# Second gate's modulation on VectorE inside the down projection, instead of on TensorE, with new queue orders

## The chip, the cores and the metric

The kernel runs on one core of one Trainium2 chip. A core has five engines that run side by side and wait for each other by semaphores: TensorE (PE, matrix products; its weight loads are shown apart as PEld), VectorE (DVE), ScalarE (ACT), GpSimd (POOL) and SyncE (SP), which here issues the DMA transfers. The metric is the device time of one execution in microseconds (us), lower is better.

## What is computed

One layer of a hybrid diffusion backbone on 128 context tokens and 512 latent tokens, with a model width D of 1024 and a feed-forward width of 2816. The input vectors `c` (latent) and `c_ctx` (context) are turned into six modulation vectors of 1024 each; the last one, `g2`, scales the output of the feed-forward part. Cut to what matters here:

```python
mod = silu(cond) @ w_ada + b_ada              # cond: c for latent tokens, c_ctx for context tokens
sh1, sc1, g1, sh2, sc2, g2 = split(mod, 6)
...                                           # token mixing: input projection, SSD and convolution, output projection
x = x + g1 * rms_norm(mix, norm_mix_post)

h = rms_norm(x, norm_ffn_pre) * (1 + sc2) + sh2
up = h @ w_ffn_up                             # 1024 -> 5632
up = depthwise_conv3x3(up)                    # latent tokens on a grid of 8 x 64; context: 3 taps in a row
f_gate, f_val = split(up, 2)
f = (silu(f_gate) * f_val) @ w_ffn_down       # 2816 -> 1024
x = x + g2 * rms_norm(f, norm_ffn_post)
```

So `g2` is used only at the very end, where the feed-forward output is scaled, and as a vector per kind of token.

## The kernel before

**Layout.** Channels lie on the 128 partitions, the 640 tokens (512 latent, then 128 context) along the free axis. The model width is 8 tiles of 128, the feed-forward width 22 tiles. Columns are handled in two halves where a norm forces it: 384 first, 256 last (`HC`). All products are made of two-part operands: a number is split into a high part (a rounded copy, made by ACT) and a low part (the rest, a subtraction by POOL or DVE), and three products high x high, high x low, low x high are added up in PSUM (`mm3`).

**Weights** come in units of 128 x 1024 or 128 x 768. For each unit SP issues one load into a tile `wr` (two buffers, L287), ACT makes `wh` (L311), POOL makes `wl` (L313). Units are numbered in order of use: `wr67` is the third unit of the up projection, `wr121` the first unit of output tile 4 of the down projection (tiles are counted from 0).

**Modulation.** `ada_first` and `ada_half` make it on PE: the weights of 512 outputs (8 tiles of 128x512, loaded by `ada_load`, L452) are multiplied by silu(c) and silu(c_ctx) in 32 matmuls (L460; two rows of the trace each), copied by ACT (L463), transposed by PE (L423), and added to the bias by DVE (L432) into `modv`. Halves 6 and 7 are `g2`. In the kernel before, half 6 is made in the up projection's head, half 7 after its unit 11.

**Up projection** (about 485 to 840 us). The head takes five units, first for the first 384 columns, then, when the second half of the norm is done, for the last 256 (L1259); the residual's second half (`xr`, L1247) is loaded meanwhile. Then one unit after another: 48 matmuls into one of three PSUM buffers, then the 3x3 convolution straight from PSUM: ACT makes the centre tap (L1227), DVE adds eight taps and two more for the context (L1237, L1239, L1240). `finish` multiplies gate and value (L1333, L1339); `split_f` splits the product for the down projection (L400 on ACT, L402 on DVE or POOL).

**Down projection** (about 820 to 960 us). Eight output tiles, each 22 x 3 products over the columns; PE only needs weights and the split products. The first two tiles are interleaved: their first 16 products come before the last six, since the last products are ready late. `down_out` has ACT square the result (L1412) and copy it, scaled by `gg2` (g2 times the norm's weight), into `mg` (L1418): tile 0 and 1 into slots H5 and H6, 2 and 3 into S8 and S9, 4 to 7 into S16, S17, U0 and U1.

**Tail** (960 to 979 us). For each half of the columns the sums of squares are made on PE, the root on ACT and DVE (L487, L488), spread by PE and copied by ACT into `HL` (L1437). `out_apply` multiplies each of the eight tiles by it (L1446), adds the residual (L1447) and sends the tile (L1448): tiles 0, 3 and 6 on POOL, the others on DVE.

**What sets the order.** The order of the instructions within each engine's queue (PE, DVE, ACT, POOL, SP) is written out: the table `ORDER` gives, for each engine, the numbers of its instructions (in the order in which the code makes them) in the order in which they are to be issued. An engine issues in that order and stops at the first instruction whose inputs or buffers aren't ready.

## Time and profile before

| | before |
|---|---|
| time, median of 3 runs (us) | 981.96 |
| lowest and highest | 980.89, 983.74 |
| span of the profiled execution, first to last instruction | 979.4 |
| mean granted TensorE clock | 0.996 |
| busy: PE, PEld, DVE, ACT, POOL (us) | 944.5, 920.9, 686.9, 471.3, 577.9 |
| moved by DMA (MB) | 117.52 |

The profiled execution's own time is its span, 979.4, with what lies around the first and last instruction; the median of the runs is 2.6 above it. Rows of the timeline read: start in us, length in us, engine, line, operation, what it writes and reads, partitions and elements, count; in brackets the idle time of the engine before it and what ended it. Neighbouring instructions of one form are one row (x4), and its length goes from the first start to the last end. "SPq" rows are the times at which SP issues a DMA. In the windows each row is a stretch: from and to, its length, then the busy time (and count) of PE, PEld, DVE, ACT and POOL, the granted TensorE clock, the share of the DMA engines and GB/s.

### The profile page before, as it was taken

How to read it: one execution, taken by the hardware profiler on the slowest of the kernel's cores; microseconds unless marked ns; L12 is line 12 of the kernel's file. 1: busy time of each engine (PE TensorE's matmuls, PEld its weight loads, DVE VectorE, ACT ScalarE, POOL GpSimd, SP SyncE). 2: the span in 40 equal slices, each digit the busy share in tenths (PEclk: the TensorE clock that was granted, in tenths of full speed). 3: DMA queues.
4: the chain of work that ended last, by engine and by line, in shares of the span. 5: the costliest groups of instructions: out<-in, count | busy, mean ns of one | idle time of the engine just before them, and what ended most of it. 6: DMA issues, size and time to landing. Idle time of an engine off the chain costs nothing.

```text
span 979.4 us, 18795 instructions
## 1 busy us (share of the span) xinstructions
PE 944.5 (96%) x7623; PEld 920.9 (94%) x7623; DVE 686.9 (70%) x1076; ACT 471.3 (48%) x799; POOL 577.9 (59%) x416
## 2 busy tenths in 40 slices
PE   4999999999999999999999999999999999999995
PEld 3799999999999998998889999999999999999995
DVE  1769898999989997523585998998988898400004
ACT  4355666877668477622464852323232336322211
POOL 1334699889999882534662994444454436543434
PEclk9999999999999999999999999999999999999998
DMA  9622424433424422578662322222222231322213
GB/s 347 250 72 86 117 82 127 146 95 123 139 80 142 128 91 93 196 244 303 200 218 88 129 86 69 84 78 73 86 66 86 66 87 54 94 69 76 82 38 108
DMA packets 50294, 117.52 MB, mean 120 GB/s; under 512 B 6016, under 2 KB 13952, under 8 KB 50208
## 3 DMA queue, kind: packets, MB, share of 16 engines
q1 hardware_dynamic: 50208, 116.33, 37.2%
q8 instruction: 60, 0.98, 0.4%
q14 instruction: 26, 0.21, 0.1%
HBM read 112.55 MB, written 3.75 MB: 119 GB/s over the span
## 4 chain that ended last, share of the span: by engine, by line
PE 87%; DMA 3%; ACT 3%; DVE 2%; SPq 1%; POOL 1%; issue 1%; POOLq 0%; ACTq 0%; DVEq 0%
PE ps L415 72%; PE ps L1259 3%; PE pq L415 2%; PE pq L818 2%; PE pq L807 1%; PE pq L460 1%; SPq L452 1%; DMA wr<-in_wout 1%; PE pq L744 1%; PE pq L441 1%; POOL wl L313 1%; PE pq L473 1%; DMA S<-acD 1%; ACT wh L311 1%; DMA T<-in_wada 1%
## 5 line engine op out<-in xcount | busy, mean ns | idle before, releaser
L313 POOL TENSOR_TENSOR wl<-wr,wh 128x1024 fp32r<-128x1024 f32 (+3 forms) x127 | 290.4, 2290 | 316.3 <-ACT wh L311 299.2
L415 PE MATMUL ps<-H,wh 128*128 128x384 f32 (+1 forms) x1636 | 315.7, 309 | 0.1
L311 ACT ACTIVATE wh<-wr 128x1024 fp32r<-128x1024 f32 (+3 forms) x131 | 131.3, 1003 | 316.2 <-PE ps L415 183.2
L415 PE MATMUL ps<-T,wh 128*128 128x384 f32 (+1 forms) x1472 | 272.5, 306 | 1.8 <-ACT S L1227 1.8
L1237 DVE SCALAR_TENSOR_TENSOR S<-ps,prms,S 128x441 f32<-128x441 f32 (+2 forms) x336 | 233.5, 695 | 29.4 <-ACT S L1227 18.9
L415 PEld LDWEIGHTS ps<-H,wh 128*128 128x128 f32 x1636 | 249.0, 188 | 2.7 <-issue 1.7
L415 PEld LDWEIGHTS ps<-T,wh 128*128 128x128 f32 x1472 | 218.9, 188 | 2.2 <-ACT S L1227 2.1
L872 DVE SCALAR_TENSOR_TENSOR ps<-u,prms,ps 128x655 f32<-128x655 f32 x205 | 185.1, 903 | 10.8 <-ACT ps L869 4.8
L415 PE MATMUL ps<-H,wl 128*128 128x384 f32 (+1 forms) x818 | 191.8, 309 | 0.0
L415 PE MATMUL ps<-T,wl 128*128 128x384 f32 (+1 forms) x736 | 166.2, 305 | 0.0
L415 PEld LDWEIGHTS ps<-H,wl 128*128 128x128 f32 x818 | 129.0, 188 | 1.0 <-issue 1.0
L415 PEld LDWEIGHTS ps<-T,wl 128*128 128x128 f32 x736 | 113.0, 188 | 0.0
L488 DVE RECIPROCAL rsm<-rsm 128x160 f32<-128x160 f32 (+2 forms) x9 | 7.4, 817 | 147.1 <-ACT rsm L487 147.1
L415 PE MATMUL ps<-S,wh 128*128 128x384 f32 (+1 forms) x420 | 88.0, 310 | 1.6 <-ACT wh L311 1.6
L415 PEld LDWEIGHTS ps<-S,wh 128*128 128x128 f32 x420 | 66.5, 188 | 2.8 <-ACT wh L311 1.8
L415 PE MATMUL ps<-S,wl 128*128 128x384 f32 (+1 forms) x210 | 54.9, 309 | 0.3 <-POOL wl L313 0.3
L789 ACT ACTIVATE S<-S,AC 128x128 f32<-128x128 f32 x140 | 45.5, 392 | 2.4 <-DMA S<-acD 2.4
L885 POOL TENSOR_TENSOR T<-T,T 128x640 f32<-128x640 f32 x20 | 32.0, 1602 | 12.5 <-ACT T L881 12.5
L1227 ACT ACTIVATE S<-ps,prms 128x640 f32<-128x640 f32 x42 | 36.5, 869 | 0.0
L415 PEld LDWEIGHTS ps<-S,wl 128*128 128x128 f32 x210 | 35.2, 188 | 0.9 <-POOL wl L313 0.5
L881 ACT ACTIVATE T<-u,prms 128x512 f32<-128x512 f32 (+1 forms) x54 | 27.9, 554 | 6.8 <-POOL T L885 6.8
L1339 POOL TENSOR_TENSOR H<-S,S 128x640 f32<-128x640 f32 x16 | 25.3, 1581 | 0.0
(346 smaller groups left out, 1180.3 us busy)
## 6 DMA issues: line engine op xcount, KB each, us to landing
wr<-in_wup SPq DMA_DIRECT2D x44, 512.0 KB, 3.5
wr<-in_win SPq DMA_DIRECT2D x36, 512.0 KB, 3.9
T<-in_wada SPq DMA_DIRECT2D x49, 256.0 KB, 5.4
S<-acD SPq DMA_DIRECT2D x28, 320.0 KB, 4.7
wr<-in_wdown SPq DMA_DIRECT2D x16, 512.0 KB, 3.4
wr<-in_wout SPq DMA_DIRECT2D x13, 512.0 KB, 4.5
H<-in_wada SPq DMA_DIRECT2D x23, 256.0 KB, 4.6
S<-in_wada SPq DMA_DIRECT2D x16, 256.0 KB, 5.4
```

The source lines that it names most:

```text
L311: ac.activation(hi[:, :n], raw[:, :n], AF.Copy)
L313: lo_eng.tensor_tensor(lo[:, :n], raw[:, :n], hi[:, :n].bitcast(F32), SUB)
L415: last_mm[0] = te.matmul(out, w, x[:, c0:c1], start=first and i == 0, stop=last and i == 2)
L789: ac.activation(rc, rc, AF.Relu, scale=-1.0, bias=AC2[:, c, row:row + 1])
L818: te.matmul(py[64 * h:64 * h + 64, i * P:(i + 1) * P], xt[:, c * P + 64 * h:c * P + 64 * h + 64], rs[h, d][:, c * P:(c + 1) * P], start=d ...
L872: ve.scalar_tensor_tensor(acc, u[:, j:j + UO], w(j), acc, MUL, ADD)
L881: ac.activation(t[:, b:c], u[:, a:a + c - b], AF.Copy, scale=w(j))
L885: gp.tensor_tensor(far, far, t, ADD)
L1227: ac.activation(out, v, AF.Identity, bias=prm_col("ffn_b", i), scale=w(1, 1))
L1237: ve.scalar_tensor_tensor(ob, vl[:, r0 + a - 1:r1 + a - 1, q0 + b - 1:q1 + b - 1], w(a, b), ob, MUL, ADD)
L1259: te.matmul(pt[:, o:o + c1 - c0], w[k] if i in (1, 2) else w[:, k * P:(k + 1) * P], x[:, c0:c1], start=k == 0 and j == 0, stop=k == KD - 1 ...
L1339: gp.tensor_tensor(f_raw[q], a, b, MUL)
```

## The change

The two last calls of `ada_half` (6 and 7) and their loads go. Instead:

- `w_ada`'s columns of g2 are laid out transposed in memory, one row of 1024 inputs per output channel, as two tiles of 128x512 for each of the eight output tiles.
- `cond_rows`, called in the up projection, loads c and c_ctx as rows broadcast to all 128 partitions (four transfers of 128x512 into S16, S17, U0 and U1) and has ACT make their silu.
- `gate_load(m)` loads the two weight tiles of output tile m: tile 0 into H5 and H6, the others into S8 and S9, one after the other. `gate_rows(m)` has DVE multiply them by the rows and sum along the free axis (`accum_out`): four operations of 128x512, then two small ones for bias and norm weight. It then issues the loads of tile m + 1.
- These are called from the down projection when its weight units come up (units 1, 3, 4, 5, 6 and 7 in `DOWN_ORDER`).
- The tables of `ORDER` are written anew from the up projection on, for DVE, ACT, POOL and SP also where nothing was added. PE's order stays as it was, apart from the matmuls that go.

```diff
-    sy.dma_start(ids, idhl_d)
+    sy.dma_start(ids, idhl_d[0:P, :])
...
-    ada_w2 = ada_load(6, [f"S{k}" for k in range(8)])
...
-    ada_half(6, ada_w2)
...
+    def cond_rows():
+        for c in range(2):
+            for h in range(2):
+                t = slot(("S16", "S17", "U0", "U1")[2 * c + h])[:, 0:512]
+                src = idhl_d[P + 32 * c + 16 * h:P + 32 * c + 16 * h + 16, :].rearrange("a b -> (a b)")
+                sy.dma_start(t, src.unsqueeze(0).to_broadcast([P, 512]))
+                ac.activation(t, t, AF.Silu)
+                crows.append(t)
...
-        if i == 11:
-            g2_rest = ada_half(7, ada_w2, now=False)
-        if i == 14:
-            g2_rest()
-        if i == 5:
-            ada_w2 = ada_load(7, [f"H{8 + k}" for k in range(8)])
+        if i == 32:
+            cond_rows()
...
-    ve.tensor_tensor(gg2, modv[:, 40:48, :], prm_col("g_ffn_post", 0, 8).unsqueeze(2).to_broadcast([P, 8, 2]), MUL)
+    junk = sm.tile([P, T], F32, tag="tanh", name="junk", bufs=1)
+    gate_ws = []
+
+    def gate_load(m):
+        ws = []
+        for h in range(2):
+            t = slot((("S8", "S9") if m else ("H5", "H6"))[h])
+            sy.dma_start(t[:, 0:512], wada2[6 + m // 4, 2 * (m % 4) + h])
+            ws.append(t)
+        gate_ws.append(ws)
+
+    def gate_rows(m):
+        for c in range(2):
+            for h, w in enumerate(gate_ws[m]):
+                ve.scalar_tensor_tensor(junk[:, 0:512], w[:, 0:512], 1.0, crows[2 * c + h], MUL, MUL,
+                                        accum_out=modv[:, 2 * m + h, c:c + 1])
+        ve.scalar_tensor_tensor(modv[:, 40 + m, :], modv[:, 2 * m, :], prm_col("b_ada", 40 + m), modv[:, 2 * m + 1, :],
+                                ADD, ADD)
+        ve.tensor_scalar(gg2[:, m, :], modv[:, 40 + m, :], prm_col("g_ffn_post", m), None, MUL)
+        if 0 < m < KD - 1:
+            gate_load(m + 1)
...
+                i = DOWN_ORDER.index((m, g))
+                if i == 1:
+                    gate_load(0)
+                    gate_load(1)
+                for j in {3: (0,), 4: (1,), 5: (2, 3), 6: (4, 5), 7: (6, 7)}.get(i, ()):
+                    gate_rows(j)
...
+    g2 = a["w_ada"][0][:, 5 * D:].T.reshape(KD, P, 2, 512).transpose(0, 2, 1, 3).reshape(2, KD, P, 512)
+    out["wada2"] = np.concatenate([w2[0:6], g2])
```

Of the tables in `ORDER`, one line of SP's:

```diff
-275 277 279 284 281 283 285-343 345 344 346 348 347 349 351 350 353 352 354 356 355 357 359 358""",
+348 357-358 360-361 363 351 354 356 359 362""",
```

What the tables do at three places follows; the numbers at the names tell buffers apart, and line numbers of the changed kernel are one higher here (L288 for L287, L403 for L402, L1479 and L1480 for L1446 and L1447).

SP's queue at the start of the up projection, before. `wr66` to `wr69` are weight units, `xr` the residual's second half, `S1` to `S3` weights of half 6 of the modulation.

```order
L452 DMA S1_636_5941<-in_wada2 128x512 [waits DMAHW3_49]
L287 DMA wr66_5893<-in_wup 128x1024 [waits DMAHW0_49,Activation_49,Pool_49]
L287 DMA wr67_5955<-in_wup 128x1024 [waits DMAHW1_49,Pool_49]
L1247 DMA xr_626_5926<-in_xT 128x2x256 [waits PE_49]
L1247 DMA xr_628_5930<-in_xT 128x2x256 [waits DMAHW7_49,PE_49]
L1247 DMA xr_627_5928<-in_xT 128x2x256 [waits PE_49]
L287 DMA wr68_5961<-in_wup 128x1024 [waits DMAHW4_49,Pool_49]
L287 DMA wr69_5971<-in_wup 128x1024 [waits DMAHW5_49,DMAHW2_49,Pool_49]
```

The same place in the changed kernel:

```order
L288 DMA wr65_5878<-in_wup 128x1024 [waits DMAHW6_49,DMAHW1_49,Pool_49]
L288 DMA wr66_5893<-in_wup 128x1024 [waits DMAHW0_49,DMAHW2_49,Activation_49,Pool_49]
L1248 DMA xr_626_5926<-in_xT 128x2x256 [waits DMAHW3_49,PE_49]
L1248 DMA xr_628_5930<-in_xT 128x2x256 [waits PE_49]
L1248 DMA xr_627_5928<-in_xT 128x2x256 [waits PE_49]
L288 DMA wr67_5939<-in_wup 128x1024 [waits DMAHW1_49,Pool_49]
L288 DMA wr68_5945<-in_wup 128x1024 [waits DMAHW7_49,DMAHW2_49,Pool_49]
L288 DMA wr69_5955<-in_wup 128x1024 [waits DMAHW6_49,Pool_49]
```

The load of `wr67` now stands behind the three of `xr`; the loads of half 6 are gone.

DVE's queue at the end of the up projection, before: the end of the convolution into S11, four low parts (the right operands H2, H4, H0 and H8 are the high parts), and the start of the last convolution, into S13.

```order
L1239 SCALAR_TENSOR_TENSOR S11_807_9251<-ps0_797_9131,prms_105,S11_807_9251 128x127
L1240 SCALAR_TENSOR_TENSOR S11_807_9251<-ps0_797_9131,prms_105,S11_807_9251 128x127 [waits DVE_49]
L402 TENSOR_TENSOR H3_817_9281<-H10_756_8027,H2_816_9279 128x640 [waits Activation_49]
L402 TENSOR_TENSOR H7_819_9285<-H11_761_8164,H4_818_9283 128x640 [waits Activation_49]
L402 TENSOR_TENSOR H1_821_9289<-H12_766_8301,H0_820_9287 128x640 [waits Activation_49,Pool_49]
L402 TENSOR_TENSOR H9_823_9293<-H13_771_8438,H8_822_9291 128x640 [waits DMAHW0_49,Activation_49,Pool_49]
L1237 SCALAR_TENSOR_TENSOR S13_824_9295<-ps1_798_9186,prms_105,S13_824_9295 128x7x63 [waits PE_49]
```

The same place in the changed kernel (`junk` is the accumulation of gate 0; the six taps between the first and the last into S13 are left out):

```order
L1410 SCALAR_TENSOR_TENSOR junk_9239,modv_123<-H5_825_9304,S16_754_8399 128x512 [waits DMAHW5_49]
L403 TENSOR_TENSOR H3_801_9185<-H10_736_7919,H2_800_9183 128x640 [waits Activation_49]
L403 TENSOR_TENSOR H7_803_9189<-H11_741_8056,H4_802_9187 128x640 [waits Activation_49]
L403 TENSOR_TENSOR H1_805_9193<-H12_746_8193,H0_804_9191 128x640 [waits Activation_49,Pool_49]
L1238 SCALAR_TENSOR_TENSOR S13_808_9199<-ps1_782_9090,prms_105,S13_808_9199 128x7x63 [waits PE_49,Activation_49]
L1238 SCALAR_TENSOR_TENSOR S13_808_9199<-ps1_782_9090,prms_105,S13_808_9199 128x7x63 [waits DVE_49]
L403 TENSOR_TENSOR H9_807_9197<-H13_751_8330,H8_806_9195 128x640 [waits DMAHW6_49,Activation_49,Pool_49]
```

Gate 0's first accumulation now stands ahead of the low parts, and H9 has moved from ahead of the last convolution to behind its eight taps.

POOL's queue in the tail, before: for each half tiles 0 (H5), 3 (S9) and 6 (U0), multiplied by the norm (`HL`) and added to the residual (`M`).

```order
L1446 TENSOR_TENSOR H5_841_9598<-H5_841_9598,HL_865_10558 128x384 [waits DVE_49,Activation_49]
L1447 TENSOR_TENSOR H5_841_9598<-H5_841_9598,M0_516_4951 128x384 [waits Pool_49]
L1446 TENSOR_TENSOR S9_848_9960<-S9_848_9960,HL_865_10558 128x384 [waits DVE_49]
L1447 TENSOR_TENSOR S9_848_9960<-S9_848_9960,M3_552_5214 128x384 [waits Pool_49]
L1446 TENSOR_TENSOR U0_857_10431<-U0_857_10431,HL_865_10558 128x384
L1447 TENSOR_TENSOR U0_857_10431<-U0_857_10431,M6_583_5506 128x384 [waits Pool_49]
L1446 TENSOR_TENSOR H5_841_9598<-H5_841_9598,HL_865_10558 128x256 [waits Activation_49]
L1447 TENSOR_TENSOR H5_841_9598<-H5_841_9598,M0_516_4951 128x256 [waits Pool_49]
L1446 TENSOR_TENSOR S9_848_9960<-S9_848_9960,HL_865_10558 128x256
L1447 TENSOR_TENSOR S9_848_9960<-S9_848_9960,M3_552_5214 128x256 [waits Pool_49]
L1446 TENSOR_TENSOR U0_857_10431<-U0_857_10431,HL_865_10558 128x256
L1447 TENSOR_TENSOR U0_857_10431<-U0_857_10431,M6_583_5506 128x256 [waits Pool_49]
```

The same place in the changed kernel:

```order
L1479 TENSOR_TENSOR H5_831_9526<-H5_831_9526,HL_865_10542 128x384 [waits DVE_49,Activation_49]
L1479 TENSOR_TENSOR S9_848_9944<-S9_848_9944,HL_865_10542 128x384 [waits DVE_49]
L1479 TENSOR_TENSOR U0_857_10415<-U0_857_10415,HL_865_10542 128x384
L1480 TENSOR_TENSOR H5_831_9526<-H5_831_9526,M0_516_4951 128x384 [waits Pool_49]
L1479 TENSOR_TENSOR H5_831_9526<-H5_831_9526,HL_865_10542 128x256 [waits Activation_49]
L1479 TENSOR_TENSOR S9_848_9944<-S9_848_9944,HL_865_10542 128x256
L1479 TENSOR_TENSOR U0_857_10415<-U0_857_10415,HL_865_10542 128x256
L1480 TENSOR_TENSOR S9_848_9944<-S9_848_9944,M3_552_5214 128x384 [waits Pool_49]
L1480 TENSOR_TENSOR U0_857_10415<-U0_857_10415,M6_583_5506 128x384 [waits Pool_49]
L1480 TENSOR_TENSOR H5_831_9526<-H5_831_9526,M0_516_4951 128x256 [waits Pool_49]
L1480 TENSOR_TENSOR S9_848_9944<-S9_848_9944,M3_552_5214 128x256 [waits Pool_49]
L1480 TENSOR_TENSOR U0_857_10415<-U0_857_10415,M6_583_5506 128x256 [waits Pool_49]
```

The multiplications now stand together, and the additions of S9 and U0 for the first 384 columns have moved behind the three multiplications of the last 256. DVE's queue has the same form (five multiplications, five additions, for each half), and SP sends POOL's last five tiles after all of DVE's.

## The prediction

> **What bounds the kernel now.** I read the shares of busy time first, then the chain that ended last, the windows by stage, and PE's waits.

> ```profile
> PE 944.5 (96%) x7623; PEld 920.9 (94%) x7623; DVE 686.9 (70%) x1076; ACT 471.3 (48%) x799; POOL 577.9 (59%) x416
> ...
> PE 87%; DMA 3%; ACT 3%; DVE 2%; SPq 1%; POOL 1%; issue 1%; POOLq 0%; ACTq 0%; DVEq 0%
> ```

> ```profile
> 700.00:790.00 90.00, 90.00 (x629) 90.00 (x628) 79.96 (x131) 28.25 (x33) 42.42 (x21) 1.00 0.25 77
> ...
> 850.00:960.00 110.00, 110.00 (x775) 109.72 (x773) 0.00 (x0) 25.72 (x37) 44.77 (x23) 1.00 0.23 67
> 960.00:979.00 19.00, 9.34 (x85) 8.83 (x81) 11.62 (x22) 3.13 (x8) 12.05 (x12) 0.81 0.40 139
> ```

> ```profile
> PE pq L481 <- DVE rsm L488: 1.5, 1, 1.5
> PE pq L473 <- ACT AT L1412: 0.5, 1, 0.5
> ```

> The windows (length, then busy PE, PEld, DVE, ACT, POOL) say that PE is full through the up projection (90.00 of 90) and the down projection (110.00 of 110), and DVE idle in the latter (0.00). The waits are those of PE from 545 to 975: two, both in the norm at the end. So until 960 each microsecond taken from PE counts, and each wait given to PE costs; after 960 DVE, POOL and SP set the end.

> The span is 979.4, the median of the runs 981.96, 2.6 above it. I count differences in the span and add them to the median. 0.3% is 2.95 us: faster is below 979.0, slower above 984.9; less can't be told from no change.

> **1. PE work removed: -4.2.**

> ```profile
> 517.24 1.18 PE L460 MATMUL pq<-S,cts 128*32 128x128 f32 x34
> ...
> 522.32 1.07 PE L460 MATMUL pq<-S,cts 128*32 128x128 f32 x28
> ...
> 591.21 1.96 PE L460 MATMUL pq<-H,cts 128*32 128x128 f32 x64
> ...
> 596.26 0.27 PE L423 MATMUL pq<-csts,adar 128*128 128x128 f32 x1
> ```

> The two last calls of `ada_half` go. The rows of 517.24 and 522.32 are the first call (its matmuls stand between others on PE), that of 591.21 the second. A matmul row's length holds about 0.1 in which the next one already runs (each group's start below is earlier than the end of the one ahead of it), so they cost 1.1 + 1.0 + 1.9 = 4.0; the two transposes, 0.27 each and overlapped too, 0.1 each. Between 4.0 and 4.75 (the whole rows and two whole transposes): I take -4.2. Both calls lie where PE is the chain. ACT's two copies, DVE's additions and 16 SP loads of 256 KB go with them; nothing in the chain waited for those.

> **2. wr67 behind the three xr loads on SP: +2.1.**

> ```profile
> 494.90 2.94 SPq L287 DMA_DIRECT2D wr<-in_wup  x2
> 498.27 1.41 SPq L1247 DMA_DIRECT2D xr<-in_xT  x3
> ```

> ```profile
> 501.88 1.05 ACT L311 ACTIVATE wh<-wr 128x1024 fp32r<-128x1024 f32 x1
> ```

> ```profile
> 503.03 0.42 PE L1259 MATMUL ps<-T,wh 128*128 128x384 f32 x1
> ```

> ```profile
> wr<-in_wup SPq DMA_DIRECT2D x44, 512.0 KB, 3.5
> ```

> ```profile
> DMA to landing us min/median/max: 3.5/3.9/4.1
> ```

> wr67 is the second of the two wr: issued at about 497.5, landed (3.5) at 501.0, split by ACT until 502.93, used by PE at 503.03: no reserve. Behind the xr loads (256 KB each; their landing is the last row) it is issued at 498.27 + 1.41 = 499.7. It lands at 503.2 if it goes at 3.5 again, and at 503.8 to 504.1 if the xr loads delay it as it delayed them (3.9 to 4.1, and a little more for its double size). With 1.05 for ACT, PE starts at 504.3 to 505.2: +1.2 to +2.2. All four share one queue, and before it was the later ones that were late, so I take 2.1, near the upper end. The xr loads themselves only get earlier.

> **3. ACT's order at the second half: -0.95.**

> ```profile
> 534.03 1.06 ACT L311 ACTIVATE wh<-wr 128x1024 fp32r<-128x1024 f32 x1 [3.60 <-issue]
> 535.00 0.87 ACT L1227 ACTIVATE S<-ps,prms 128x640 f32<-128x640 f32 x1
> ```

> ```profile
> 535.90 5.81 DVE L1237 SCALAR_TENSOR_TENSOR S<-ps,prms,S 128x441 f32<-128x441 f32 x8 [4.23 <-ACT S L1227]
> ...
> 542.00 0.35 DVE L1240 SCALAR_TENSOR_TENSOR S<-ps,prms,S 128x127 f32<-128x127 f32 x1
> ```

> ```profile
> 542.49 0.82 PE L415 MATMUL ps<-T,wh 128*128 128x384 f32 x4 [1.76 <-ACT S L1227]
> ```

> PE waits 1.76 for a PSUM buffer whose reader, the first convolution, began behind L1227, which stood behind a weight split. Now L1227 comes first: 535.00 - 534.03 = 0.97 earlier. The DVE convolution is long (6.5) and PE still waits, so all of it counts; bounds 0 to -1.0.

> **4. H9 behind a convolution on DVE: +2.0.** At the end of the up projection the low part of feed-forward tile 15 (H9, with H8) was made before the last convolution; now behind its eight taps, and an accumulation of gate 0 is put ahead.

> ```profile
> 811.63 3.40 DVE L402 TENSOR_TENSOR T<-H,T 128x640 fp32r<-128x640 f32 x4 [3.05 <-ACT T L400]
> ...
> 821.32 7.49 DVE L402 TENSOR_TENSOR H<-H,H 128x640 fp32r<-128x640 f32 x4
> 828.73 5.80 DVE L1237 SCALAR_TENSOR_TENSOR S<-ps,prms,S 128x441 f32<-128x441 f32 x8
> ```

> ```profile
> 819.89 2.42 POOL L313 TENSOR_TENSOR wl<-wr,wh 128x1024 fp32r<-128x1024 f32 x1
> ```

> ```profile
> 830.30 0.75 PE L415 MATMUL pq<-H,wh 128*128 128x384 f32 x4
> ```

> Four splits cost 3.40 alone and 7.49 beside POOL. PE, by steps 1 to 3 about 3.1 early, reaches H9 at 830.30 - 3.1 = 827.2. DVE: the four splits at 811.63 move into the convolution behind them, so the 3.05 of idle time goes: 821.3 - 3.1 - 3.05 = 815.1; four two-input operations beside POOL 7.5, eight taps 5.8, H9 0.85: 829.2. So +2.0. With 3.4 for the four there is no wait; with the idle time kept, 5: bounds 0 to +5. 7.5 is the row of this very place.

> **5. The tail: +3.5.** Before, DVE and POOL multiply, add and send one tile after another. Now all multiplications come first, and two of POOL's additions of the first columns (384) stand behind its three multiplications of the last (256), where SP's last five sends are POOL's.

> ```profile
> 971.31 0.38 ACT L1437 ACTIVATE HL<-pq 128x256 f32<-128x256 f32 x1 [2.22 <-PE pq L481]
> ```

> ```profile
> 970.12 1.25 POOL L1447 TENSOR_TENSOR U<-U,M 128x384 f32<-128x384 f32 x1
> 971.77 0.73 POOL L1446 TENSOR_TENSOR H<-H,HL 128x256 f32<-128x256 f32 x1 [0.40 <-ACT HL L1437]
> ...
> 976.03 0.79 POOL L1447 TENSOR_TENSOR U<-U,M 128x256 f32<-128x256 f32 x1
> ```

> ```profile
> 969.58 0.54 DVE L488 RECIPROCAL rsm<-rsm 128x64 f32<-128x64 f32 x1
> ...
> 972.18 0.59 DVE L1447 TENSOR_TENSOR H<-H,M 128x256 f32<-128x256 f32 x1
> ```

> Before, POOL's last addition ends at 976.82. Now, from 971.77: three multiplications, 3 x 0.8 = 2.4; additions 2 x 1.25 + 3 x 0.79, with gaps 5.0; end 979.2, +2.4. But DVE's five additions now stand back to back beside POOL's; if each holds POOL for 0.5, on POOL's 0.73 alone (1.0 for 384, estimated by size): 2.4 + 4.2 + 2.5 = 9.1, 980.9, +4.0. I take the middle, +3.2. Then DVE's reciprocal of the second half (before at 969.58, between its operations) now stands behind five multiplications and five additions: at 0.54 and 0.5 to 0.8 each from 963.9, 969.1 to 970.6, so HL comes 0.5 earlier to 1.0 later: +0.3. Sum +3.5, bounds +1.9 to +5.0. SP isn't the bound: a send takes about 0.4, a POOL addition 0.73 or more. [...]

> **6. Added and hidden: 0.** Four broadcast loads and four ACT Silu fall into the up projection, where ACT is busy 28.25 of 90; laid open, four operations of the size of ACT's 0.93 below would be at most 3.7. 32 accumulating DVE operations of 128x512 with 16 small ones fall into the down projection; 16 loads of 256 KB go onto SP among the wdown loads. Nearest row:

> ```profile
> L574 DVE SCALAR_TENSOR_TENSOR S<-tanh,S 128x640 f32<-128x640 f32 x6 | 4.9, 824 | 1.3 <-ACT tanh L573 1.3
> ```

> By size 0.69, with the sum 0.75: 24 us where DVE has 110 idle. Were none of it hidden it would be all 24. Not free is the chain: from gate 2 on a load into S8/S9 waits until DVE has read the gate before; and ACT's write of S8 for output tile 2 waits for gate 7, with weight split wh121 behind it on ACT.

> ```profile
> 872.13 0.93 ACT L1418 ACTIVATE S<-ps,gg 128x512 f32<-128x512 f32 x2
> 877.68 1.06 ACT L311 ACTIVATE wh<-wr 128x1024 fp32r<-128x1024 f32 x1 [4.62 <-issue]
> ```

> ```profile
> 839.77 48.71 SPq L287 DMA_DIRECT2D wr<-in_wdown  x9
> ```

> ```profile
> 878.82 2.41 POOL L313 TENSOR_TENSOR wl<-wr,wh 128x1024 fp32r<-128x1024 f32 x1 [3.71 <-ACT wh L311]
> ```

> ```profile
> 890.36 0.45 PE L415 MATMUL ps<-S,wl 128*128 128x384 f32 x2
> ```

> ```profile
> DMA to landing us min/median/max: 2.6/4.3/6.2
> ```

> The last row is of the gate weights' loads before (line 452). A turn takes a landing of 2.6 (the queue is light), three operations 2.4 and 1 of issue and POOL: 6.0. From 845 (gate 1 read) six turns end at 881. Then 0.7 + 1.06 + 2.41 give wl121 at 885.2, PE needs it at 890.36 less what it is early: 4.8 in reserve, 0.8 a turn. On SP one wdown load stands behind each waiting pair; they go out one a turn of 6.0, and before nine went in 48.71, one in 6.1. Hidden.

> **Sum.** -4.2 + 2.1 - 0.95 + 2.0 + 3.5 + 0 = +2.45: span 981.8 against 979.4, time 984.4.

> **Rivals.**
> - *The waits don't come.* wr67 lands early enough (+1.2), DVE's four operations miss POOL (0), the tail is at its lower bound (+1.9): -4.2 - 0.95 + 3.1 = -2.05, 979.9; with the tail level too, 978.0; with none of the three, 976.8. The point that decides is the tail, the largest term: below +1 with the others at their lower bounds the kernel is faster. For it: POOL's last six operations keep their number and kind. Against: POOL's idle time ahead of the last half now holds none of the two moved additions, and the rows of steps 2 and 4 are of these very places. Chance 0.17, of it 0.115 faster and 0.055 within 0.3%.
> - *The gate chain overruns.* Above 1.0 an operation, or 3.4 a landing, the reserve is gone; at the median landing of 4.3 six turns are 10.2 longer, 5.4 past the reserve: 989.5. Against: 4.3 comes from eight loads at once. [...] Chance 0.14, all slower.
> - *The change doesn't pay in PE.* The first removed half only lengthens the wait at 542.49, if DVE or ACT set its time rather than PE: -2.1 falls out, 986.5. Against: DVE stood idle 4.23 for ACT, and ACT waited for PE there. Chance 0.04, slower.

> **Chances.** My forecast's case has 0.65, with its own range 981.5 to 987.0; by the open sizes of steps 2, 4 and 5 about 0.02 of it lies below 979.0, 0.42 above 984.9, the rest between. Faster 0.115 + 0.015 = 0.13; slower 0.65 x 0.42 + 0.14 + 0.04 = 0.45; same 0.42. The range runs from 980.0, about the first rival's first form, to 988.0, short of the chain's 989.5; outside lie most of 0.115 and part of 0.14.

> **What would show it.** Step 1: no L460 behind 510. Step 2: a PE wait of about 2 before its first matmul on wh67. Step 3: the wait at the restart near 1. Step 4: PE waiting for DVE's H9 near 829. Step 5: more than 8 us between ACT's last HL and POOL's last addition, against 5.5. Step 6: accumulating operations near 0.75, and no PE wait near 890. It is wrong if PE doesn't wait at 2 and 4, or does at 6.

## The result, and the profile after

The changed kernel takes 995.33 us (median of 4 runs, 994.72 to 1000.99) against 982.85 before; the ratio is 1.0142, 95% interval 1.0114 to 1.0171. 984.4 had been forecast, with 988.0 as the upper end: it is slower, and by far more.

The longest waits of PE in the changed kernel, from 480 us to the end (total, times, longest); the line numbers are one higher than before:

```profile
PE pq L416 <- DVE H L403: 4.7, 1, 4.7
PE ps L1260 <- ACT wh L312: 3.1, 1, 3.1
PE pq L482 <- DVE rsm L489: 3.0, 2, 1.8
PE ps L416 <- ACT wh L312: 1.7, 1, 1.7
PE ps L416 <- DVE S L1241: 0.9, 1, 0.9
```

The first is H9 at the end of the up projection, the second wr67, both where the prediction had put them. This is what came behind them, in PE's timeline and in the windows (PE busy, PEld, DVE, ACT, POOL, then the granted clock):

```profile
507.70 0.69 PE L1260 MATMUL ps<-T,wh 128*128 128x384 f32 x1 [3.08 <-ACT wh L312]
508.19 0.52 PE L1260 MATMUL ps<-T,wl 128*128 128x384 f32 x1
...
836.02 0.90 PE L416 MATMUL pq<-H,wh 128*128 128x384 f32 x2 [4.75 <-DVE H L403]
836.72 0.74 PE L416 MATMUL pq<-H,wl 128*128 128x384 f32 x2
...
842.69 0.46 PE L416 MATMUL ps<-T,wl 128*128 128x384 f32 x2
```

```profile
507.70:511.10 3.40, 3.40 (x11) 3.40 (x12) 3.40 (x5) 2.51 (x5) 3.37 (x3) 0.51 0.03 11
836.00:842.00 6.00, 5.98 (x22) 5.98 (x23) 5.96 (x6) 0.84 (x1) 4.36 (x2) 0.50 0.30 87
```

The same pair of matmuls takes 0.74 at 836.7 and 0.46 at 842.7. For 3.4 us behind the first wait and 6.0 behind the second the granted clock is 0.5. The waits were paid twice: once idle, once at half clock.

Where the 14.2 us between the two spans (993.6 and 979.4) went is read by setting the start of the same matmul in both traces against each other. The changed kernel is 1.4 behind at 487, where the two programs are still the same; 4.7 at the first matmul on wr67; 6.2 when the clock is back; 3.9 without the first half of g2; 3.0 at the second half's restart; 0.5 without the second half of g2, and steady there to 820; 5.4 at H9; 8.6 shortly after the clock is back, steady to 960; 14.2 at the end. The 1.4 of the start is no work of the change: the profiled runs of the kernels below differ from before by -2.6 to +2.0 there, with the same program.

The accumulations in the down projection:

```profile
L1410 DVE SCALAR_TENSOR_TENSOR junk<-S,U x14: 691/692/693, 849.7 to 885.9; 128x512 f32<-128x512 f32 x14
```

```profile
L1410 DVE DVE_READ_ACCUMULATOR junk<-S,U x14: 80/82/84, 850.4 to 886.5; 128x1 f32 x14
```

```profile
850.00:960.00 110.00, 110.00 (x762) 110.00 (x761) 32.37 (x66) 28.00 (x41) 49.77 (x24) 1.00 0.33 99
```

692 ns and 82 for reading the sum, 0.77 together; PE is full there all the same (110.00 of 110, DVE now 32.37).

The tail: the second HL on ACT, DVE's last addition, POOL's last addition, and SP's last sends.

```profile
981.10 0.38 ACT L1470 ACTIVATE HL<-pq 128x256 f32<-128x256 f32 x1 [3.40 <-PE pq L482]
```

```profile
986.98 0.94 DVE L1480 TENSOR_TENSOR U<-U,M 128x256 f32<-128x256 f32 x1
```

```profile
985.88 0.90 POOL L1480 TENSOR_TENSOR H<-H,M 128x256 f32<-128x256 f32 x1
...
987.60 0.90 POOL L1480 TENSOR_TENSOR U<-U,M 128x256 f32<-128x256 f32 x1
```

```profile
987.98 0.33 SPq L1481 DMA_DIRECT2D out_yT<-U  x1
...
990.40 0.38 SPq L1481 DMA_DIRECT2D out_yT<-U  x1
```

From HL to POOL's last addition it is 7.4 us (988.5 less 981.1) against 5.5 before, and SP sends for 2.3 more: it stood at DVE's last tile until 987.98, while four of POOL's tiles were ready, and then had five to send, one every 0.5 us.

### The profile page after: what moved, and what is told of

The parts are those of the page before. It is cut to its first block, busy times and chain, and to the rows that moved or that the text cites. A ratio compares the mean times of both kernels' runs of the same rounds, so it can differ in the third digit from the quotient of the medians.

```text
span 993.6 us, 18616 instructions
## 1 busy us (share of the span) xinstructions
PE 945.6 (95%) x7493; PEld 921.8 (93%) x7493; DVE 732.7 (74%) x1151; ACT 473.6 (48%) x801; POOL 577.4 (58%) x416
## 4 chain that ended last, share of the span: by engine, by line
PE 80%; DVE 7%; DMA 6%; ACT 3%; POOL 1%; issue 1%; SPq 1%; POOLq 0%; ACTq 0%; DVEq 0%
PE ps L416 68%; DVE S L1238 4%; PE ps L1260 3%; DMA T<-in_wada 2%; PE pq L819 2%; PE pq L808 1%; DMA wr<-in_wout 1%; DVE H L403 1%; PE pq L745 1%; DMA S<-acD 1%; POOL wl L314 1%; ACT wh L312 1%; DMA S<-in_wada 1%; PE pq L416 1%; PE pq L442 1%
## 5 line engine op out<-in xcount | busy, mean ns | idle before, releaser
L416 PE MATMUL ps<-H,wh 128*128 128x384 f32 (+1 forms) x1636 | 315.7, 309 | 0.1
L416 PE MATMUL ps<-T,wh 128*128 128x384 f32 (+1 forms) x1472 | 273.8, 307 | 0.9 <-DVE S L1241 0.9
L416 PEld LDWEIGHTS ps<-H,wh 128*128 128x128 f32 x1636 | 249.1, 188 | 2.6 <-issue 2.1
L416 PEld LDWEIGHTS ps<-T,wh 128*128 128x128 f32 x1472 | 220.4, 189 | 1.1 <-ACT S L1228 1.1
L416 PE MATMUL ps<-H,wl 128*128 128x384 f32 (+1 forms) x818 | 191.6, 309 | 0.0
L416 PE MATMUL ps<-T,wl 128*128 128x384 f32 (+1 forms) x736 | 167.0, 307 | 0.0
L416 PEld LDWEIGHTS ps<-H,wl 128*128 128x128 f32 x818 | 129.0, 188 | 1.0 <-issue 1.0
L416 PEld LDWEIGHTS ps<-T,wl 128*128 128x128 f32 x736 | 113.7, 189 | 0.0
L416 PE MATMUL ps<-S,wh 128*128 128x384 f32 (+1 forms) x420 | 87.8, 310 | 1.7 <-ACT wh L312 1.7
L416 PEld LDWEIGHTS ps<-S,wh 128*128 128x128 f32 x420 | 66.5, 188 | 2.7 <-ACT wh L312 1.9
L416 PE MATMUL ps<-S,wl 128*128 128x384 f32 (+1 forms) x210 | 54.7, 308 | 0.5 <-POOL wl L314 0.5
L416 PEld LDWEIGHTS ps<-S,wl 128*128 128x128 f32 x210 | 35.2, 188 | 0.9 <-POOL wl L314 0.7
## 6 DMA issues: line engine op xcount, KB each, us to landing
wr<-in_wup SPq DMA_DIRECT2D x44, 512.0 KB, 3.6
wr<-in_win SPq DMA_DIRECT2D x36, 512.0 KB, 3.9
wr<-in_wdown SPq DMA_DIRECT2D x16, 512.0 KB, 3.5
wr<-in_wout SPq DMA_DIRECT2D x13, 512.0 KB, 4.0
```

Source lines behind the costliest of these rows:

```text
L416: last_mm[0] = te.matmul(out, w, x[:, c0:c1], start=first and i == 0, stop=last and i == 2)
```

## The experiments

Three edits undo one new order each, and a fourth kernel has all three; the gate on DVE stays in all of them. The kernels with the tail's order of before have line numbers two lower than the changed kernel's (L414 for L416, L401 for L403); the diffs of the tables show only the numbers around the edit.

**wr67 ahead of the xr loads again.** In SP's table:

```diff
-258 260 259 262 263      (xr, xr, xr, wr67, wr68)
+262 258 260 259 263      (wr67, xr, xr, xr, wr68)
```

> The changed kernel with one edit: SP issues wr67 ahead of the three xr loads again. Theory A (a long PE wait costs itself and then slow matmuls: behind the 3.08 us wait at 507.7 the granted clock is 0.51 for 3.4 us): the wait goes and 1.2 us of slow matmuls with it, less the 0.5 us that stood there before; about 4.3 us faster than the changed kernel, 991.0, and the clock between 503 and 511 reads 1.0. Theory B (the matmuls behind the wait are slow for a reason of their own): 3.1 us faster at most, 992.2, the clock still near 0.5 there. Theory C (another wait takes its place: the norm of the second half comes no earlier): no difference, 995.

Measured: 987.08 us, ratio to before 1.0044 (1.0027 to 1.0061). PE doesn't wait, and the clock is whole:

```profile
503.00:511.00 8.00, 8.00 (x46) 7.81 (x46) 7.97 (x20) 3.36 (x7) 5.01 (x5) 1.00 0.37 122
```

From 487 to 820 PE gains 5.6 on before, against 0.9 in the changed kernel: 4.7 from this edit, 3.3 of wait and 1.5 of slow clock, as theory A has it. The medians differ by 8.2; of the rest 1.6 is in H9's wait and the tail, which are shorter in this trace (7.3 lost at H9 instead of 8.1), and some 2 lies ahead of the edit, where the programs are the same. B and C fall.

**H9 ahead of the last convolution again.** In DVE's table (1032 is H9, 1033 to 1040 are the taps):

```diff
-1049 1029-1031 1033-1040 1032 1041-1042
+1049 1029-1031 1032 1033-1040 1041-1042
```

> The changed kernel with one edit: H9 is made ahead of the last convolution again, right behind H1; gate 0's first accumulation stays where it is. Theory A: the 4.75 us wait shrinks below 1 us, and the 6 us at a granted clock of 0.50 behind it, which cost 3.1 us, go too: 7 to 8 us faster, 987.5 to 988.5. Theory B: only the wait goes, 4 to 4.7 us, 991. Theory C (DVE is late in all it does here and the next low parts make PE wait as long): within 1 us of 995.

Measured: 989.79 us, ratio 1.0079 (1.0050 to 1.0109), 5.5 less than the changed kernel. The wait for H9 is gone; a later one of 0.9 is left there. The wait for wr67 stays in this kernel. In the trace PE loses 1.6 on before between 798 and 851, against 8.1: 6.5 less. With the interval of the ratio (2.9 us to either side) the medians don't separate A from B here; the trace does, since the clock from 835 to 842 is 1.00 in this kernel:

```profile
835.00:842.00 7.00, 6.98 (x49) 6.72 (x47) 7.00 (x5) 0.74 (x1) 6.64 (x3) 1.00 0.44 114
```

**The tail's order of before** on DVE, POOL and SP (tile by tile: multiply, add, send; SP's line is left out here):

```diff
 DVE:  -1098 1100 1102 1104 1106 1099 1101 1103 1105 1107-1109 1111 1113 1115 1117 1110 1112 1114 1116 1118
       +1098-1106 1108 1107 1109-1118
 Pool: -400 402 404 401 406 408 410 403 405 407 409 411
       +400-411
```

> The changed kernel with one edit: DVE, POOL and SP have the tail's order of before (multiply, add, send, tile by tile). The part of the tail from ACT's second HL on goes back from about 9.3 us to the last send to 5.5, and the norm's 1.2 us extra ahead of HL (0.3 for the reciprocal behind DVE's additions, 0.9 for PE's spread at a granted clock of 0.5) go mostly: 4.5 to 5.5 us faster, 990 to 991. [...]

Measured: 989.18 us, ratio 1.0071 (1.0049 to 1.0093), 6.1 less than the changed kernel. From the first HL to the end it is 16.7 us, against 21.6 in the changed kernel and 16.1 before. So 4.9 of 5.5 come back with the order; the 0.6 that doesn't come back lies behind the last send and is not explained. The profiled spans differ by more, 7.0: in this run the wait for H9, 4.74 long where it was 4.75 in the changed kernel, was followed by only 3.4 us at half clock, and PE lost 6.4 there instead of 8.1.

**All three.**

> All three edits together. Theory A with no interplay: 995.3 - 4.3 - 7.5 - 5.0 = 978.5, which is the removed PE work (4.4) and ACT's order (0.9) as a gain over before, ratio 0.995 to 0.996. Theory B: 995.3 - 3.1 - 4.4 - 5 = 982.8, no difference from before. Theory C (gate accumulations or their loads cost something that the waits hid): 983 or more.

Measured: 978.83 us, ratio 0.9947 (0.9930 to 0.9964), faster than both kernels, at the value that theory A gives. PE's waits between 510 and 950:

```profile
PE pq L414 <- DVE S L401: 0.9, 1, 0.9
PE ps L414 <- DVE S L1239: 0.9, 1, 0.9
```

From 487 to 820 PE gains 5.7 on before: the removed PE work and ACT's order, 4.2 and 0.95 by the prediction. Near 843 it loses 1.2 again, 0.9 of it the first wait above, for a low part. So the gate on DVE costs little, and the three new orders had turned a gain into a loss.

**A longer gate chain.** To this kernel a fifth accumulation was added for gates 1 to 7:

```diff
+        if m:
+            ve.scalar_tensor_tensor(junk[:, 0:512], gate_ws[m][1][:, 0:512], 1.0, crows[3], MUL, MUL,
+                                    accum_out=modv[:, 2 * m + 1, 1:2])
```

> The kernel with all three edits, and a fifth accumulation of 128x512 on DVE for gates 1 to 7 (the fourth one repeated). It asks how much the chain of gate loads and accumulations has in reserve. In the kernel with three edits ACT writes S8 at 880.7, wh121 and wl121 follow by 884.8, and PE needs wl121 at about 885: no reserve left, by that reading. Six turns get 0.77 longer each, 4.6 in all: PE waits 4 to 5 us for wl121, with 2 us of slow matmuls behind it: 985 to 986. If the turn is bound by the load's landing and not by DVE, or the chain has a reserve elsewhere: no difference, 979.

Measured: 985.27 us, ratio 1.0010 (0.9990 to 1.0030), 6.4 more than without it, as the first reading has it:

```profile
PE ps L414 <- ACT wh L310: 2.6, 1, 2.6
PE ps L414 <- POOL wl L312: 1.0, 1, 1.0
```

PE loses 6.5 on before between 860 and 893: 3.6 of waits and 2.9 of slow clock, which stands behind these two waits as well:

```profile
892.00:895.00 3.00, 3.00 (x13) 3.00 (x12) 0.00 (x0) 0.65 (x1) 1.43 (x1) 0.50 0.73 171
895.00:898.00 3.00, 3.00 (x23) 3.00 (x22) 0.00 (x0) 1.62 (x4) 2.73 (x2) 1.00 0.37 141
```

Without the fifth accumulation POOL is done with wl121 at 884.83 and PE takes it at 885.48: 0.65 in reserve, so the expectation's reading of none was nearly right. In the changed kernel the reserve was 8.9 (890.04 and 898.98), since PE came so much later.

**How long a wait must be.** H9 was put behind 4, 5 and 6 of the taps in the kernel with all three edits.

```diff
+1049 1029-1031 1033-1036 1032 1037-1042      (4 taps; then 1033-1037 1032, 1033-1038 1032)
```

> The kernel with all three edits, but H9 behind four taps: PE waits about 1.9 us. Waits of 2.60 and 3.30 at this place were followed by a granted clock of 0.5 for about 3.4 and 5.6 us; the 1.76 of before, at 542, by none. Theory A3 (a window of a fixed length looks for idle time; a wait that fills too little of it changes nothing): the clock stays at 1.0, and PE is about 1 us later than in the kernel with three edits, which waits 0.9 a little later anyway. If a wait of any length did it, a slow stretch of 3 us, 1.5 more.

> The kernel with all three edits, but H9 behind five of the last convolution's eight taps: PE waits about 2.7 us for it. It asks how long a wait must be to be followed by slow matmuls. Theory A1 (only waits over about 3 us): the granted clock behind the wait stays at 1.0 and the wait costs 2.7 and no more. Theory A2 (every wait does it, in proportion): the clock reads 0.5 for 2 to 3 us, 1.2 more.

> The same with H9 behind six taps: PE waits about 3.5 us. Theory A1: the granted clock behind the wait is 0.5 for 3 to 6 us, and PE is 1.5 to 3 us later than the wait alone makes it. Theory B (the slow matmuls of the changed kernel came from what DVE and POOL did at the time): the clock stays at 1.0.

Measured, one run each: 981.48, 980.90 and 985.24. Single runs differ by 2 us and more in stretches with the same program, so the traces count. The first matmul behind the wait, and the clock from there, for 4, 5 and 6 taps:

```profile
830.18 0.55 PE L414 MATMUL pq<-H,wh 128*128 128x384 f32 x2 [1.82 <-DVE H L401]
```

```profile
830.00:832.00 2.00, 1.82 (x12) 1.82 (x13) 1.93 (x4) 0.85 (x1) 0.00 (x0) 1.00 0.00 0
832.00:834.00 2.00, 2.00 (x16) 2.00 (x15) 1.93 (x5) 0.00 (x0) 0.29 (x1) 1.00 0.00 0
```

```profile
827.95 0.56 PE L414 MATMUL pq<-H,wh 128*128 128x384 f32 x2 [2.60 <-DVE H L401]
```

```profile
827.90:829.50 1.60, 1.55 (x8) 1.54 (x9) 1.53 (x3) 0.84 (x1) 0.00 (x0) 0.78 0.00 0
829.50:831.00 1.50, 1.50 (x8) 1.50 (x7) 1.47 (x4) 0.00 (x0) 0.30 (x1) 0.50 0.00 0
831.00:833.00 2.00, 2.00 (x11) 2.00 (x10) 2.00 (x2) 0.00 (x0) 2.00 (x2) 0.70 0.27 52
```

```profile
830.40 0.90 PE L414 MATMUL pq<-H,wh 128*128 128x384 f32 x2 [3.30 <-DVE H L401]
```

```profile
834.00:836.00 2.00, 2.00 (x9) 2.00 (x9) 2.00 (x2) 0.00 (x0) 2.00 (x2) 0.50 0.43 131
836.00:838.00 2.00, 2.00 (x15) 2.00 (x15) 2.00 (x2) 0.86 (x2) 0.80 (x1) 0.96 0.61 158
```

The wait of 1.82 is followed by no slow clock (PE loses 2.1 in all), that of 2.60 by some 3.4 us at 0.5 (4.4 lost), that of 3.30 by 5.7 (6.2 lost). Theory A1 put the limit too high; B falls, since the clock is 0.5 behind waits made here too. After the wait of 2.60 the first 0.8 us still run at full clock; the drop comes later.

By these three alone the limit would lie between 1.8 and 2.6 us. Two other waits on record don't fit that. In the kernel with H9 alone put back the wait for wr67 has the clock whole behind it:

```profile
507.52 0.44 PE L1260 MATMUL ps<-T,wh 128*128 128x384 f32 x1 [3.14 <-ACT wh L312]
```

```profile
507.00:511.00 4.00, 3.48 (x20) 3.48 (x21) 4.00 (x7) 3.03 (x6) 3.45 (x3) 1.00 0.08 26
```

In the kernel with 5 taps a wait of 1.74, ahead of the up projection, is followed by half clock:

```profile
482.76 0.50 PE L414 MATMUL ps<-S,wh 128*128 128x256 f32 x2 [1.74 <-ACT wh L310]
```

```profile
484.10:487.40 3.30, 3.30 (x17) 3.30 (x17) 3.30 (x5) 0.69 (x2) 1.25 (x2) 0.50 0.63 195
```

What decides in these runs is where the idle time falls. Within each trace the granted clock changes only at times that lie whole multiples of 3.41 us apart; in the changed kernel these are 507.62, 511.03, 835.30, 842.12 and 978.66. Divided into such steps of 3.41 us, as far as the clock is recorded (in the changed kernel from 19.5 us on), all twelve traces say the same: each of the 26 steps at full clock in which PE was idle for 1.81 us or more is followed by half clock. Of the steps with 1.74 to 1.80 idle three are and two are not, and of all those with 1.70 or less only two are (1.44 and 1.33), which stays open. The clock came back behind the first step in which PE was idle for 0.29 or less, and stayed low with 0.68 or more. The wait of 3.14 lay in two steps, with 1.44 idle in the one and 1.70 in the other; that of 1.74 lay in one. So the limit that the runs show is on the idle share of one step, about half of it (idle time is taken from the profile's modelled ends of matmuls), and a wait of a given length can come out either way.

**SP's order in the tail alone**, on the changed kernel: POOL's sends stand between DVE's, as they come ready.

> The changed kernel with one edit: SP's sends in the tail stand in the order in which DVE's and POOL's tiles come ready by its trace; DVE and POOL keep their new order. In the changed kernel POOL's last addition ended at 988.5 and SP issued the last of five sends in a row at 990.4. If SP's order is what ends last, the last send now follows POOL's last addition within 0.5: 1.5 us less from the second HL to the end. If POOL's additions are what ends last, no difference there.

Measured, one run: 993.36 us. The second HL on ACT, POOL's last addition and SP's last sends:

```profile
980.63 0.38 ACT L1470 ACTIVATE HL<-pq 128x256 f32<-128x256 f32 x1 [3.39 <-PE pq L482]
```

```profile
987.14 0.90 POOL L1480 TENSOR_TENSOR U<-U,M 128x256 f32<-128x256 f32 x1
```

```profile
987.86 0.89 SPq L1481 DMA_DIRECT2D out_yT<-U  x2
```

The last send ends 8.1 us behind HL's start (988.75 less 980.63), against 9.7 in the changed kernel (990.78 less 981.10): 1.6 less. So SP's order ended last by that much, as expected, and POOL's last addition, 7.4 behind HL in both kernels against 5.5 before, makes the rest.

**A try beyond.** In the kernel with all three edits the two accumulations on a gate's first weight tile come first (the loop over tiles outside that over the two vectors), and gate 0's first one stands behind the low parts.

> A try at a better version: the kernel with all three edits; in each gate the two accumulations that read the first weight tile come first, so that its slot is free one accumulation earlier, and gate 0's first accumulation stands behind the low parts at the end of the up projection. It should take the 0.9 us that PE waits for a low part there, and shorten the turn of the gate chain by about 0.8 us, so that ACT's wait for S8 shrinks by some 4 us. PE doesn't wait for that chain in the kernel with three edits, so only the 0.9 counts: 977.9 to 978.8, a difference that can't be told for sure. If the moved accumulation makes the chain late instead: a PE wait near wl121 and 980 or more.

Measured: 979.02 us, ratio 0.9960 (0.9944 to 0.9976). The wait of 0.9 fell to 0.3 and ACT's for S8 from 10.75 to 9.46 us, less than the 4 that was expected; PE loses 1.2 between 820 and 860 in both kernels, and the time can't be told from 978.83.

## Why the prediction was wrong, point by point

- **Step 1 (PE work, -4.2): right.** With step 3, 5.15 was forecast; between 512 and 820 PE gains 5.4 to 5.7 on before in the traces of all the changed kernels.
- **Step 2 (wr67, +2.1): right place, too small, 3.3 and 1.5 more of slow clock.** The load landed 5.3 us after its issue, not 4.4:

```profile
499.67 1.40 SPq L1248 DMA_DIRECT2D xr<-in_xT  x3
501.17 3.69 SPq L288 DMA_DIRECT2D wr<-in_wup  x2
```

```profile
506.60 1.06 ACT L312 ACTIVATE wh<-wr 128x1024 fp32r<-128x1024 f32 x1 [3.21 <-DMA wr<-in_wup]
```

  The step took xr's delay as a measure. An estimate made afterwards goes by bytes: 0.79 MB of xr and 0.52 MB of wr67 at 261 GB/s (last column below) are 5.0 us from the first xr's issue, which gives 504.7; the 1.8 left until 506.5 would be issue and landing. No run tests this split:

```profile
503.00:507.50 4.50, 1.62 (x13) 1.39 (x11) 4.50 (x11) 1.29 (x2) 1.50 (x1) 1.00 0.86 261
```

- **Step 3 (-0.95): right,** 0.9.
- **Step 4 (H9, +2.0): right place, too small, 4.75 and 3.1 more of slow clock.** Against PE's arrival DVE's four operations began 1.3 later than forecast, and they took 9.0, not 7.5:

```profile
814.99 2.94 DVE L403 TENSOR_TENSOR T<-H,T 128x640 fp32r<-128x640 f32 x2
...
820.51 0.95 DVE L1410 SCALAR_TENSOR_TENSOR junk<-H,S 128x512 f32<-128x512 f32 x1
...
821.39 8.11 DVE L403 TENSOR_TENSOR H<-H,H 128x640 fp32r<-128x640 f32 x3
829.43 5.80 DVE L1238 SCALAR_TENSOR_TENSOR S<-ps,prms,S 128x441 f32<-128x441 f32 x8
835.15 0.81 DVE L403 TENSOR_TENSOR H<-H,H 128x640 fp32r<-128x640 f32 x1
```

  Three splits beside POOL took 8.11, 2.7 each: about POOL's own 2.2 to 3.0 for one of its operations there. And one of the splits that had moved ahead met POOL too (2.94 for two, where the step had 0.85 each), which is the 1.3. The upper bound of the step, 5, would have held the wait, not what came behind it.
- **Step 5 (tail, +3.5): too small, 5.6.** POOL's last addition came 1.9 later against HL, a little under the 2.4 to 4.0 taken, and the sign set for it, more than 8 us between the two, did not come: it is 7.4. That each of DVE's additions holds POOL for 0.5, which gave the 4.0, was the author's estimate, and the runs don't show it: POOL's five additions took 4.9 together in the changed kernel (983.61 to 988.50), against 6.7 with it and 5.0 without. But "SP isn't the bound" was wrong: SP's sends, put at nothing, make 1.6 to 1.9 (1.6 came off with their order alone). HL came 1.2 later: 0.3 by the reciprocal, as forecast, and 0.9 because PE's spread ran at a granted clock of 0.50 (its eight matmuls took 1.97, and before 1.10 at 1.00). The last 0.6 lies behind the last send and is open.
- **Step 6 (hidden): right.** An accumulation takes 0.77 where 0.75 was taken; the 0.06 in it for the sum was the author's estimate, which no row of before shows, and the read of the sum takes 0.08. The 692 ns for 512 elements are near what L574's 824 for 640, without a sum, give by size (659). No wait for wl121 stands in the trace. The step's reserve of 4.8 is a slip, since its own terms make PE 1.05 early there and leave 4.1; the rival's 989.5 would be 990.5.
- **What no step had: the clock.** All terms counted a wait of PE at its own length. Behind the two added waits the half clock cost 1.5 + 3.1, in the tail 0.9. The clock stands at 1.00 or 0.50 here and changes in steps of 3.41 us, and PE needn't be idle for a whole step: 1.81 us in one was enough each time. Since a wait may fall on one step or on two, the clock's part in the changed kernel's 14.2 is partly chance: a wait of 3.14 for wr67 cost nothing behind it in another run, and H9's cost 1.7 less.

Together: forecast +2.45 in the span, measured 14.2, and 1.4 of it is the start. The other 10.35 are 1.2 of wait and 1.5 of clock at wr67, 2.75 and 3.1 at H9 with 0.2 of other waits near it, and 2.1 in the tail (its 0.9 of clock among them), less 0.5 that steps 1 and 3 brought more than forecast. The failed steps are the sizes of 2, 4 and 5 (in 5 the sends of SP, put at nothing), and the rule under all of them that a wait costs its own length.

## What to carry to other kernels

A wait added to a full TensorE is to be priced with the clock behind it: here 1.8 us cost 2.1, 2.6 cost 4.4 and 4.75 cost 8.1. The price depends on where the wait falls on the clock's steps of 3.41 us, so it is a range and not a number: 3.1 us once cost nothing behind it, and 4.74 once cost 6.4. When a change moves work off the bound and lays the queues out anew, test the two apart: here the work moved, with ACT's new order, gained 0.5%, and three other orders cost 1.7%. A send that waits in SP's in-order queue holds all that stand behind it (here until 987.98, with four tiles ready; 1.6 came off when they were sent as they came ready), so in a tail the sends belong in the order in which their tiles come ready.
